# Summing and turning the modulation vectors of a diffusion transformer: one transposing reduction and one 0/1 matmul in place of eight TensorE instructions

## Chip, cores, metric

The kernel runs on 1 core of one Trainium2 chip. The metric is device time in microseconds (us): the median of several executions. Beside them stands one profiled execution, from which all rows below come.

## What is computed

Two layers of a transformer for a diffusion generator, on 256 latent and 256 context tokens of 1024 features. Each layer has a first FFN, a mixer (two kinds of attention and a linear recurrence) and a second FFN; each of these shifts, scales and gates its input with modulation vectors. The part that matters here:

```python
m_lat = (jax.nn.silu(c) @ ada_w[l] + ada_b[l]).reshape(b, N_MOD, d_model)
m_ctx = (jax.nn.silu(c_ctx) @ ada_w[l] + ada_b[l]).reshape(N_MOD, d_model)
...
h = ffn_step(h, ml, ffn1_w13[l], ffn1_w2[l], norm_g[l, 0], 0)
```

N_MOD is 9, d_model 1024. So for each layer and each of nine indices m there is a product of two vectors (c and c_ctx) with a 1024 x 1024 block of `ada_w`, with a bias added.

## The kernel before

Features lie on the 128 partitions, tokens along the free dimension, 512 at a time (256 context, 256 latent). Every large fp32 product is made of three fp32r matmuls: ScalarE copies a weight tile into a high half (`split`, line 353), VectorE subtracts to get the low half (line 354), and `mm3` (lines 360 to 362) adds high x high, low x high and high x low. Names tell the place: `f_0a8L` is the low half of the first-product weights of FFN 0 (the first of the layer), first of the two gate halves, feature group 8; `f_0pa` and `f_0pb` are the accumulators of the two gate halves; `f_0w_4L` is a low half of the second product's weights (`project_back`), `f_0w0y` its accumulator, `f_0gH`/`f_0gL` the halves of its input. `f_2...` is the same for the second FFN.

Two of the first layer's vectors (m = 0 and 1) are made on TensorE at the start (`ada_start`). The other 16, (0, 2) to (0, 8) and (1, 0) to (1, 8), are made on VectorE beside the FFNs (`ada_mod`): four 1 MB loads of `ada_w` on the SP queue (tile `araw`, three buffers), and for each 128 rows of the block and each of the two vectors one multiply-add over 128 x 1024 elements (lines 225 and 227) into `aacc`, one buffer. `ada_mod` is a generator; the FFN takes one step of it after each feature group. At the end of each vector:

- four matmuls with a column of ones in a 128 x 32 block (`left1`) sum the accumulator over the partitions (line 233), each writing 32 of the 128 partitions of `asum`;
- `to_mods` copies that to SBUF on ScalarE (line 180), turns it in four 128 x 128 transposes on TensorE (line 183, `ada_..t`), and two VectorE adds with the bias write 128 x 8 each into `mods` (line 188).

Then `gain` or a multiplication by 0.5 follows. A scheduler puts the instructions into the engines' queues; each engine works its queue in order. The order around the change is thus the scheduler's, from the order in the code, its priorities and its own estimates of durations.

`rsqrt` (line 251) makes the small reciprocal roots of the norms, in a tile `r` of three buffers. `shape_constants` builds the table of constants, which is loaded at the start on the SP queue, the first 128 columns by themselves.

Of the kernel before, what the change touches and what calls it, by code (L numbers as in the profile page):

```python
# [10 lines left out]
F32 = mybir.dt.float32  # L11
F32R = mybir.dt.float32r
AF = mybir.ActivationFunctionType
ALU = mybir.AluOpType
AX = mybir.AxisListType
# [11 lines left out]
EPS = 1e-6  # L27
GRID_W = 64
THETA = 10000.0
C_IDENT, C_COS, C_SIN, C_LDA, C_LGQ = 0, 128, 384, 640, 768  # L30
C_ALL = 864
HALVES = ((0, 0, 256), (1, 256, 512))
FSPLIT = (0, 12, 22)
TAGS = {'e': 5, 'p': 5, 'v': 4, 'Q': 5, 'K': 4, 'o': 8, 'T': 6}
# [2 lines left out]
def shape_constants():  # L37

    out = np.zeros((128, C_ALL), np.float32)
    out[:, C_IDENT:C_IDENT + 128] = np.eye(128, dtype=np.float32)  # L40
    half = HD // 4
    inv = (np.float32(THETA) ** (-np.arange(half, dtype=np.float32) / np.float32(half))).astype(np.float32)
    t = np.arange(SEQ)
    pos = np.stack([t // GRID_W, t % GRID_W]).astype(np.float32)
    for p in range(128):
        axis, i = (p // 32) % 2, p % 16
        ang = (pos[axis] * inv[i]).astype(np.float32)
        out[p, C_COS:C_COS + SEQ] = np.cos(ang)
        out[p, C_SIN:C_SIN + SEQ] = np.sin(ang) * (-1.0 if p % 32 < 16 else 1.0)
    for h in range(4):  # L50
        out[:, C_LDA + 32 * h + h] = 1.0
    for i in range(3):
        out[:64, C_LGQ + 32 * i + 2 * i] = 1.0
        out[64:, C_LGQ + 32 * i + 2 * i + 1] = 1.0
    return out


@with_exitstack
def hybrid_kernel(ctx: ExitStack, tc, x, c, ctx_tok, c_ctx, ada_w, ada_b, norm_g, ffn1_w13, ffn1_w2,
# [3 lines left out]
    V, S, G, PE = nc.vector, nc.scalar, nc.gpsimd, nc.tensor  # L63
# [7 lines left out]
    sml = ctx.enter_context(tc.tile_pool(name="sml", bufs=4))  # L71
# [10 lines left out]
    def tabled(out_, in_, func, **kw):  # L82
        which = {AF.Tanh: AF.Exp}.get(func, func)
        if which != table["set"]:
            table.update(set=which, before=table["last"])
        i = S.activation(out_, in_, func, **kw)  # L86
        if table["before"] is not None:
            tc.add_manual_dep(i.ins, table["before"].name,
                              mybir.DependencyInfo(mybir.DependencyClass.NoSync, mybir.DependencyReason.DATA),
                              reason="table set")  # L90
        table["last"] = i.ins

    def t512(name="t"):
        return tmp.tile([128, 512], F32, tag="t", name=name)

    def ps(name="ps", tag="ms"):
        return pss.tile([128, 512], F32, tag=tag, name=name)
# [5 lines left out]
    start = ctx.enter_context(ExitStack())  # L103
# [7 lines left out]

    cs = cp.tile([128, C_ALL], F32, name="cs")
    nc.sync.dma_start(out=cs[:, 0:128], in_=consts[:, 0:128])
# [7 lines left out]
    bT = cp.tile([128, L, 72], F32, name="bT")  # L121
# [41 lines left out]
    mods = [cp.tile([128, 72, 2], F32, name=f"mods{l}") for l in range(L)]  # L163
    gs = [cp.tile([128, 3, KD, 2], F32, name=f"gs{l}") for l in range(L)]

    def gain(l, i, k0, k1):

        n0 = col["ng"] + (3 * l + i) * KD
        V.scalar_tensor_tensor(
            gs[l][:, i, k0:k1], mods[l][:, 8 * (3 * i + 1) + k0:8 * (3 * i + 1) + k1, :], 1.0,  # L170
            vT[:, n0 + k0:n0 + k1].rearrange("p (k o) -> p k o", o=1).to_broadcast([128, k1 - k0, 2]),
            op0=ALU.add, op1=ALU.mult)

    def to_mods(l, acc, m0, mstep, c0, off, what, more=None):


        nb = len(off)
        rows_ = 128
        sb = t512(f"{what}s")
        S.activation(sb[0:rows_, :], acc[0:rows_, :], AF.Copy)  # L180
        tp = ps(f"{what}t", "tp")
        for t in range(4):
            PE.transpose(tp[:, 128 * t:128 * t + rows_], sb[0:rows_, 128 * t:128 * t + 128], ident[0:rows_, 0:rows_])
        tv = tp.rearrange("p (t r) -> p t r", t=4)
        for b in range(nb):
            q = 8 * m0 + mstep * b + c0
            st_ = off[b][1] - off[b][0]
            V.tensor_tensor(
                out=mods[l][:, q:q + 4, :], in0=tv[:, :, off[b][0]:off[b][1] + 1:st_],
                in1=bT[:, l, q:q + 4].rearrange("p (t o) -> p t o", o=1).to_broadcast([128, 4, 2]), op=ALU.add)  # L190
            if more is not None:
                V.tensor_tensor(out=mods[l][:, q:q + 4, :], in0=mods[l][:, q:q + 4, :],
                                in1=tv[:, :, off[b][0] + more:off[b][1] + more + 1:st_], op=ALU.add)

    def ada_start(pool, part, acc):

# [13 lines left out]
    def ada_started(acc, part):  # L210
        to_mods(0, acc, 0, 8, 4 * part, ((0, 1), (32, 33)), f"ada_s{part}", 64)
        gain(0, 0, 4 * part, 4 * part + 4)

    def ada_mod(pool, l, m):


        acc = pool.tile([128, 2, 1024], F32, tag="aacc", name=f"aacc{l}_{m}", bufs=1)
        for n in range(4):
            w = pool.tile([128, 2, 1024], F32, tag="araw", name=f"araw{l}_{m}_{n}")
            nc.sync.dma_start(out=w, in_=ada_w[l, 256 * n:256 * n + 256, 1024 * m:1024 * m + 1024].rearrange("(n p) c -> p n c", p=128))  # L220
            for i in range(2):
                k = 2 * n + i
                for v in range(2):
                    if k == 0:
                        V.tensor_scalar(acc[:, v], w[:, i], cpad[:, k, v:v + 1], None, op0=ALU.mult)
                    else:
                        V.scalar_tensor_tensor(acc[:, v], w[:, i], cpad[:, k, v:v + 1], acc[:, v], op0=ALU.mult, op1=ALU.add)  # L227
            yield
        sm = ps(f"asum{l}_{m}")
        for v in range(2):  # L230
            for b in range(2):
                j = 2 * b + v
                PE.matmul(sm[32 * j:32 * j + 32, :], left1, acc[:, v, 512 * b:512 * b + 512], start=True, stop=True)
        to_mods(l, sm, m, 4, 0, ((0, 32), (64, 96)), f"ada{l}_{m}")
        if m % 3 == 1:
            gain(l, m // 3, 0, KD)
        elif m != 5 and m % 3 == 2:
            V.tensor_scalar(mods[l][:, 8 * m:8 * m + 8, :], mods[l][:, 8 * m:8 * m + 8, :], 0.5, None, op0=ALU.mult)
# [3 lines left out]
    left1 = cs[:, C_LDA:C_LDA + 32]  # L242
# [5 lines left out]

    def rsqrt(st, scale, a, b, name):
        sl = slice(a // 4, b // 4)  # L250
        r = sml.tile([128, 128], F32, tag="r", name=name, bufs=3)
        tabled(r[sl], st[sl, 0:128], AF.Sqrt, bias=eps_t[sl], scale=scale)
        V.reciprocal(r[sl], r[sl])
        return r
# [13 lines left out]
    class Stat:  # L268
# [31 lines left out]
        def rstd(self, a, b):  # L300
            if self.c0:
                r = self.scales(a, b)
                bc = ps(f"bc{self.name}_{a}")
                for n in range((b - a) // 128):
                    PE.matmul(bc[:, a + 128 * n:a + 128 * n + 128], r[:, n:n + 1].to_broadcast([128, 128]), ident,
                              start=True, stop=True)
                return bc
            st = ps(f"st{self.name}_{a}", "tp")
            parts = [self.sum, self.sq[6], self.sq[7]]
            for n, sq in enumerate(parts):  # L310
                stat_mm(st, left1, sq, a, b, n == 0, n == 2)
            r = rsqrt(st, 1.0 / D, a, b, f"r{self.name}_{a}")
            return spread(ps(f"bc{self.name}_{a}"), r, 0, 1, a, b, a, b)
# [108 lines left out]
    def ffn(l, i, w13, w2, c0, nstat, adas=(), begin=None):  # L422
        nm = f"f{l}_{i}"
        with tc.tile_pool(name=f"gp{nm}", bufs=1) as gp, tc.tile_pool(name=f"ap{nm}", bufs=3) as ap:
            opening = begin is not None
            def run_adas():
                if opening:
                    small_params()
                for l_, m in adas:
                    yield from ada_mod(ap, l_, m)  # L430
# [71 lines left out]
    def mixer(l, c0, nstat):  # L502
        W = w_in[l]
        nm = f"m{l}"
        with tc.tile_pool(name=f"mp{l}", bufs=1) as mp, tc.tile_pool(name=f"mt{l}", bufs=1) as mt:
# [262 lines left out]
            def subln(heads):  # L768
                st = ps(f"{nm}ost")
                for n, h in enumerate(heads):  # L770
                    sq = t512("sq")
                    S.activation(sq[:, c0:], om[h][:, c0:], AF.Square)
                    stat_mm(st, cs[:, C_LDA + 32 * n:C_LDA + 32 * n + 32], sq, c0, NT, n == 0, n == len(heads) - 1)
                ro = rsqrt(st, 1.0 / 128, c0, NT, f"{nm}ro")
                for n, h in enumerate(heads):
                    bc = spread(ps(f"{nm}obc{h}"), ro, n, 1, c0, NT, c0, NT)
                    V.scalar_tensor_tensor(om[h][:, c0:], om[h][:, c0:], gsub[:, l:l + 1], bc[:, c0:], op0=ALU.mult, op1=ALU.mult)
# [191 lines left out]
```

## Time and profile before

| | |
|---|---|
| median of 3 runs | 1788.25 us (1787.35 to 1788.76) |
| profiled execution | 1787.78 us, of which 1786.0 us are the span of the profile |
| TensorE matmul busy | 1753.0 us, 98% |
| TensorE weight loads busy | 1465.0 us, 82% |
| VectorE busy | 1129.4 us, 63% |
| ScalarE busy | 714.0 us, 40% |
| GpSimd busy | 77.7 us, 4% |
| moved by DMA | 249.33 MB, mean 140 GB/s |

The span is the part of an execution between the first and the last instruction of the profile. Matmuls are pipelined: a row's duration is longer than the distance to the next, so the distance between starts is what a matmul costs its queue. An fp32 matmul shows as two records, an fp32 transpose or an fp32r matmul as one.

### The profile page before, as it was taken

How to read it: one execution, taken by the hardware profiler on the slowest of the kernel's cores; microseconds unless marked ns; L12 is line 12 of the kernel's file. 1: busy time of each engine (PE TensorE's matmuls, PEld its weight loads, DVE VectorE, ACT ScalarE, POOL GpSimd, SP SyncE). 2: the span in 40 equal slices, each digit the busy share in tenths (PEclk: the TensorE clock that was granted, in tenths of full speed). 3: DMA queues.
4: the chain of work that ended last, by engine and by line, in shares of the span. 5: the costliest groups of instructions: out<-in, count | busy, mean ns of one | idle time of the engine just before them, and what ended most of it. 6: DMA issues, size and time to landing. Idle time of an engine off the chain costs nothing.

```text
span 1786.0 us, 23865 instructions
## 1 busy us (share of the span) xinstructions
PE 1753.0 (98%) x9773; PEld 1465.0 (82%) x9773; DVE 1129.4 (63%) x1663; ACT 714.0 (40%) x1131; POOL 77.7 (4%) x75
## 2 busy tenths in 40 slices
PE   6999999999999999999999999999999999999998
PEld 3788888889787788878888898878888987799998
DVE  5767977337668767789566455783333777865554
ACT  3422222324677643221223342222222477754444
POOL 0000000001100010000000100000000120010001
PEclk9999999999999999999999999999999999999999
DMA  9555763233212136557355324552223322145652
GB/s 342 195 171 174 245 212 118 83 107 100 72 47 72 48 113 218 188 190 255 120 170 177 101 95 141 177 177 95 95 83 105 100 97 71 49 142 178 201 164 97
DMA packets 192822, 249.33 MB, mean 140 GB/s; under 512 B 6722, under 2 KB 170952, under 8 KB 192712
## 3 DMA queue, kind: packets, MB, share of 16 engines
q1 hardware_dynamic: 192712, 247.80, 41.6%
q8 instruction: 77, 1.26, 0.3%
q14 instruction: 33, 0.27, 0.0%
HBM read 246.73 MB, written 1.05 MB: 139 GB/s over the span
## 4 chain that ended last, share of the span: by engine, by line
PE 94%; DVE 2%; ACT 2%; issue 1%; DMA 0%; POOL 0%; SPq 0%; ACTq 0%; POOLq 0%; DVEq 0%
PE f_0pa L360 5%; PE f_0pa L361 5%; PE f_0pb L360 5%; PE f_0pa L362 5%; PE f_0pb L361 4%; PE f_0pb L362 4%; PE f_2pa L360 4%; PE f_2pb L360 3%; PE f_2pa L361 3%; PE f_2pa L362 3%; PE f_2pb L361 3%; PE f_2pb L362 3%; PE f_0w0y L360 3%; PE f_0w0y L362 2%; PE f_0w0y L361 2%; PE f_0w1y L360 2%
## 5 line engine op out<-in xcount | busy, mean ns | idle before, releaser
L227 DVE SCALAR_TENSOR_TENSOR aacc<-araw,cpad,aacc 128x1024 f32<-128x1024 f32 x224 | 275.0, 1276 | 2.8 <-DMA araw<-in_ada_w_dram 2.8
L86 ACT ACTIVATE g<-f_0pa 128x512 f32<-128x512 f32 x44 | 26.3, 598 | 153.3 <-PE f_0pa L362 153.3
L284 POOL TENSOR_TENSOR sss<-sss,sqs 128x512 f32<-128x512 f32 (+1 forms) x20 | 27.1, 1353 | 1322.4 <-ACT sqs L282 1321.7
L488 DVE TENSOR_TENSOR g<-g,f_0pb 128x512 f32<-128x512 f32 x44 | 30.1, 685 | 82.8 <-PE f_0pb L362 72.2
L354 DVE TENSOR_TENSOR f_0w_0L<-f_0w,f_0w_0H 128x1024 fp32r<-128x1024 f32 (+1 forms) x32 | 34.7, 1088 | 55.4 <-ACT f_0w_0H L353 55.3
L353 ACT ACTIVATE f_0w_0H<-f_0w 128x1024 fp32r<-128x1024 f32 (+1 forms) x32 | 30.4, 951 | 88.6 <-PE f_0w0y L362 39.8
L86 ACT ACTIVATE g<-f_2pa 128x512 f32<-128x512 f32 (+1 forms) x44 | 21.6, 490 | 106.0 <-PE f_2pa L362 106.0
L354 DVE TENSOR_TENSOR f_2w_0L<-f_2w,f_2w_0H 128x1024 fp32r<-128x1024 f32 (+1 forms) x32 | 34.9, 1089 | 36.0 <-ACT f_2w_0H L353 35.9
L326 ACT ACTIVATE xH<-xn,mods 128x256 fp32r<-128x256 f32 x88 | 39.0, 499 | 43.0 <-DVE xn L325 42.8
L353 ACT ACTIVATE f_2w_0H<-f_2w 128x1024 fp32r<-128x1024 f32 (+1 forms) x32 | 30.4, 950 | 64.2 <-PE f_2w0y L362 30.6
L360 PE MATMUL f_0w0y<-f_0gH,f_0w_0H 128*128 128x512 f32 x128 | 50.6, 397 | 0.0
L361 PE MATMUL f_0w0y<-f_0gH,f_0w_0L 128*128 128x512 f32 x128 | 50.3, 393 | 0.0
L362 PE MATMUL f_0w0y<-f_0gL,f_0w_0H 128*128 128x512 f32 x128 | 50.0, 391 | 0.0
L681 DVE TENSOR_REDUCE sm<-s 128x1 f32<-128x512 f32 (+1 forms) x72 | 42.1, 590 | 6.3 <-PE s L676 5.9
L488 DVE TENSOR_TENSOR g<-g,f_2pb 128x512 f32<-128x512 f32 (+1 forms) x44 | 24.3, 552 | 34.1 <-PE f_2pb L362 29.0
L360 PE MATMUL f_2w0y<-f_2gH,f_2w_0H 128*128 128x512 f32 (+1 forms) x128 | 43.3, 338 | 0.0
L361 PE MATMUL f_2w0y<-f_2gH,f_2w_0L 128*128 128x512 f32 (+1 forms) x128 | 43.1, 336 | 0.0
L353 ACT ACTIVATE f_0w_4H<-f_0w 128x1024 fp32r<-128x1024 f32 x16 | 17.0, 1061 | 64.7 <-PE f_0w0y L362 27.6
L362 PE MATMUL f_2w0y<-f_2gL,f_2w_0H 128*128 128x512 f32 (+1 forms) x128 | 42.8, 335 | 0.0
L360 PE MATMUL f_0w1y<-f_0gH,f_0w_0H 128*128 128x512 f32 (+1 forms) x120 | 42.4, 354 | 0.0
L362 PE MATMUL f_0w1y<-f_0gL,f_0w_0H 128*128 128x512 f32 (+1 forms) x120 | 41.6, 347 | 0.0
L361 PE MATMUL f_0w1y<-f_0gH,f_0w_0L 128*128 128x512 f32 (+1 forms) x120 | 41.6, 347 | 0.0
(1416 smaller groups left out, 5865.9 us busy)
## 6 DMA issues: line engine op xcount, KB each, us to landing
araw<-in_ada_w_dram SPq DMA_DIRECT2D x64, 1024.0 KB
f_0a<-in_ffn_w_dram SPq DMA_DIRECT2D x22, 1024.0 KB
f_0b<-in_ffn_w_dram SPq DMA_DIRECT2D x22, 1024.0 KB
f_2a<-in_ffn_w_dram SPq DMA_DIRECT2D x22, 1024.0 KB
f_2b<-in_ffn_w_dram SPq DMA_DIRECT2D x22, 1024.0 KB
f_0w<-in_ffn_w_dram SPq DMA_DIRECT2D x16, 1024.0 KB
f_2w<-in_ffn_w_dram SPq DMA_DIRECT2D x16, 1024.0 KB
adas<-in_ada_w_dram SPq DMA_DIRECT2D x16, 512.0 KB
```

The lines of the kernel that those rows point to most:

```text
L86: i = S.activation(out_, in_, func, **kw)
L227: V.scalar_tensor_tensor(acc[:, v], w[:, i], cpad[:, k, v:v + 1], acc[:, v], op0=ALU.mult, op1=ALU.add)
L284: self.adder.tensor_tensor(out=self.sum[:, a:b], in0=self.sum[:, a:b], in1=sq[:, a:b], op=ALU.add)
L326: S.activation(xH[:, k, a:b], t[:, a:b], AF.Identity, bias=sh)
L353: S.activation(vH, src, AF.Copy)
L354: V.tensor_tensor(out=vL, in0=src, in1=f32(vH), op=ALU.subtract)
L360: PE.matmul(acc, aH, bH, start=first, stop=False)
L361: PE.matmul(acc, aL, bH, start=False, stop=False)
L362: PE.matmul(acc, aH, bL, start=False, stop=last)
L488: V.tensor_tensor(out=t_[:, c0:], in0=t_[:, c0:], in1=pb[:, c0:], op=ALU.mult)
L681: V.reduce_max(st_[:, 0:1], s[:, 0:nk], axis=AX.X, negate=True)
```

## The change

The four summing matmuls, the ScalarE copy and the four transposes go. In their place one VectorE instruction transposes each 32 x 32 block of the accumulator and sums it along its rows: of 2048 values on each partition remain 64 (`red`), for each group of 32 features the sum over the 32 partitions of a quadrant. One matmul with a 0/1 matrix (`C_S32`: 4 x 4 copies of the 32 x 32 unit matrix) adds the four quadrants and puts the result on all four, and four VectorE adds with the bias, one for each quadrant, write `mods`. The constants lose two unused columns of 32 and gain the 128 columns of the 0/1 matrix; `r` has two buffers. `to_mods` stays for the two vectors of the start, with its last argument now required.

```diff
-C_IDENT, C_COS, C_SIN, C_LDA, C_LGQ = 0, 128, 384, 640, 768
-C_ALL = 864
+C_IDENT, C_COS, C_SIN, C_LDA, C_LGQ, C_S32 = 0, 128, 384, 640, 704, 800
+C_ALL = 928
...
+    out[:, C_S32:C_S32 + 128] = np.tile(np.eye(32, dtype=np.float32), (4, 4))
...
-        sm = ps(f"asum{l}_{m}")
-        for v in range(2):
-            for b in range(2):
-                j = 2 * b + v
-                PE.matmul(sm[32 * j:32 * j + 32, :], left1, acc[:, v, 512 * b:512 * b + 512], start=True, stop=True)
-        to_mods(l, sm, m, 4, 0, ((0, 32), (64, 96)), f"ada{l}_{m}")
+        red = sml.tile([128, 64], F32, tag="red", name=f"red{l}_{m}", bufs=1)
+        V.tensor_reduce(red, acc.rearrange("p v (b j) -> p (v b) j", j=32), axis=AX.X, op=ALU.add, apply_transpose=True)
+        sm = ps(f"asum{l}_{m}")
+        PE.matmul(sm[:, 0:64], cs[:, C_S32:C_S32 + 128], red, start=True, stop=True)
+        sv = sm[:, 0:64].rearrange("p (v k r) -> p k v r", v=2, r=4)
+        for r in range(4):
+            q = slice(32 * r, 32 * r + 32)
+            V.tensor_tensor(
+                out=mods[l][q, 8 * m:8 * m + 8, :], in0=sv[q, :, :, r],
+                in1=bT[q, l, 8 * m:8 * m + 8].rearrange("p (k o) -> p k o", o=1).to_broadcast([32, 8, 2]), op=ALU.add)
...
-        r = sml.tile([128, 128], F32, tag="r", name=name, bufs=3)
+        r = sml.tile([128, 128], F32, tag="r", name=name, bufs=2)
```

The change also moves instructions. On TensorE, in the second product of layer 0's first FFN, at the end of vector (0, 4), the queue before reads:

```order
L362 MATMUL f_0w0y_1_0_1330<-f_0gL_304,f_0w_8_0H 128x512
L233 MATMUL asum_4_1409<-aacc_4_1225,cs 32x512 x4
L360 MATMUL f_0w0y_0_0_1451<-f_0gH_303,f_0w_0_0H 128x512
L361 MATMUL f_0w0y_0_0_1451<-f_0gH_303,f_0w_0_0L 128x512
L362 MATMUL f_0w0y_0_0_1451<-f_0gL_304,f_0w_0_0H 128x512
L360 MATMUL f_0w0y_1_0_1452<-f_0gH_303,f_0w_0_0H 128x512
L183 MATMUL ada_4t<-cs,ada_4s 128x128 x4
L361 MATMUL f_0w0y_1_0_1452<-f_0gH_303,f_0w_0_0L 128x512
```

And now, in the changed program, whose lines are five further down there:

```order
L367 MATMUL f_0w0y_1_0_1318<-f_0gL_304,f_0w_8_0H 128x512
L233 MATMUL asum_4_1399<-red_4_1397,cs 128x64
L365 MATMUL f_0w0y_0_0_1433<-f_0gH_303,f_0w_0_0H 128x512
L366 MATMUL f_0w0y_0_0_1433<-f_0gH_303,f_0w_0_0L 128x512
L367 MATMUL f_0w0y_0_0_1433<-f_0gL_304,f_0w_0_0H 128x512
L365 MATMUL f_0w0y_1_0_1434<-f_0gH_303,f_0w_0_0H 128x512
L366 MATMUL f_0w0y_1_0_1434<-f_0gH_303,f_0w_0_0L 128x512
```

The one matmul stands where the four stood, and the transposes are gone; the same holds at the other vectors.

On VectorE, around the start of that second product (the lines of `f_0w_..L` are the splits, `g` and `f_0gL` close a feature group of the first product, `aacc` are the vectors' multiply-adds), the queue before reads:

```order
L354 TENSOR_TENSOR f_0w_0_0L<-f_0w_0_1301,f_0w_0_0H 128x1024
L488 TENSOR_TENSOR g<-g,f_0pb_1181 128x512
L225 TENSOR_SCALAR aacc_4_1225<-araw_4_0_1226,cpad 128x1024
L490 TENSOR_TENSOR f_0gL_304<-g,f_0gH_303 128x512
L188 TENSOR_TENSOR mods_115<-ada_3t,bT 128x8 x2
L227 SCALAR_TENSOR_TENSOR aacc_4_1225<-araw_4_0_1226,cpad,aacc_4_1225 128x1024 x2
L227 SCALAR_TENSOR_TENSOR aacc_4_1225<-araw_4_1_1295,cpad,aacc_4_1225 128x1024 x4
L227 SCALAR_TENSOR_TENSOR aacc_4_1225<-araw_4_2_1303,cpad,aacc_4_1225 128x1024 x2
L488 TENSOR_TENSOR g<-g,f_0pb_1265 128x512
L354 TENSOR_TENSOR f_0w_0_4L<-f_0w_0_1301,f_0w_0_4H 128x1024
L227 SCALAR_TENSOR_TENSOR aacc_4_1225<-araw_4_3_1319,cpad,aacc_4_1225 128x1024 x4
L354 TENSOR_TENSOR f_0w_8_0L<-f_0w_8_1317,f_0w_8_0H 128x1024
```

And now:

```order
L227 SCALAR_TENSOR_TENSOR aacc_4_1213<-araw_4_3_1307,cpad,aacc_4_1213 128x1024 x3
L359 TENSOR_TENSOR f_0w_0_0L<-f_0w_0_1289,f_0w_0_0H 128x1024
L493 TENSOR_TENSOR g<-g,f_0pb_1175 128x512
L237 TENSOR_TENSOR mods_115<-asum_3_1207,bT 32x16 x4
L359 TENSOR_TENSOR f_0w_0_4L<-f_0w_0_1289,f_0w_0_4H 128x1024
L495 TENSOR_TENSOR f_0gL_304<-g,f_0gH_303 128x512
L231 TENSOR_REDUCE red_4_1397<-aacc_4_1213 128x64
L225 TENSOR_SCALAR aacc_5_1406<-araw_5_0_1407,cpad 128x1024 x2
L227 SCALAR_TENSOR_TENSOR aacc_5_1406<-araw_5_0_1407,cpad,aacc_5_1406 128x1024
L359 TENSOR_TENSOR f_0w_8_0L<-f_0w_8_1305,f_0w_8_0H 128x1024
```

Vector (0, 4)'s multiply-adds are done before the product starts, and the next vector's begin there; both splits have fewer of them in front. (Of the first list, rows between the ones shown are left out.)

## Rows read from the trace of the kernel before

**Rows 1.** The page, its first lines: span and busy time of each engine.
```profile
span 1786.0 us, 23865 instructions
...
PE 1753.0 (98%) x9773; PEld 1465.0 (82%) x9773; DVE 1129.4 (63%) x1663; ACT 714.0 (40%) x1131; POOL 77.7 (4%) x75
```
**Rows 2.** The page, the chain that ended last, by engine.
```profile
PE 94%; DVE 2%; ACT 2%; issue 1%; DMA 0%; POOL 0%; SPq 0%; ACTq 0%; POOLq 0%; DVEq 0%
```
**Rows 3.** Windows: length, busy time per engine, clock, DMA share, GB/s.
```profile
60.00:345.00 285.00, 285.00 (x1282) 229.40 (x1281) 205.99 (x251) 83.40 (x106) 0.00 (x0) 1.00 0.51 171
690.00:960.00 270.00, 270.00 (x1217) 217.52 (x1216) 199.27 (x215) 72.37 (x90) 0.00 (x0) 1.00 0.56 189
1060.00:1215.00 155.00, 155.00 (x703) 124.35 (x702) 103.41 (x114) 41.75 (x52) 0.00 (x0) 1.00 0.48 159
sum 710.00, PE 710.00 PEld 571.26 DVE 508.67 ACT 197.51 POOL 0.00; mean PE 236.67 PEld 190.42 DVE 169.56 ACT 65.84 POOL 0.00
```
**Rows 4.** Tile asum, TensorE: count, ns min/median/max, first and last start.
```profile
L233 PE MATMUL asum<-aacc,cs x128: 592/605/617, 121.0 to 1201.5; 128*32 128x512 f32 x128
```
**Rows 5.** Timeline of TensorE, vector (0, 4): start us, us, instruction.
```profile
194.96 0.40 PE L362 MATMUL f_0w0y<-f_0gL,f_0w_0H 128*128 128x512 f32 x1
195.28 1.06 PE L233 MATMUL asum<-aacc,cs 128*32 128x512 f32 x8
...
196.62 0.39 PE L361 MATMUL f_0w0y<-f_0gH,f_0w_0L 128*128 128x512 f32 x1
196.85 0.39 PE L362 MATMUL f_0w0y<-f_0gL,f_0w_0H 128*128 128x512 f32 x1
197.09 0.39 PE L360 MATMUL f_0w0y<-f_0gH,f_0w_0H 128*128 128x512 f32 x1
197.32 0.60 PE L183 MATMUL ada_4t<-cs,ada_4s 128*128 128x128 f32 x4
...
197.99 0.39 PE L362 MATMUL f_0w0y<-f_0gL,f_0w_0H 128*128 128x512 f32 x1
```
**Rows 6.** Timeline, TensorE, mixer of layer 0: two fp32 matmuls among weight matmuls.
```profile
594.93 0.40 PE L361 MATMUL m0oy<-xH,m0o_0L 128*128 128x512 f32 x1
...
595.16 0.64 PE L758 MATMUL o<-m0pT,m0v 128*128 128x128 f32 x4
...
595.88 0.28 PE L675 MATMUL s<-m0K,m0Q 128*128 128x256 f32 x1
```
**Rows 7.** Timeline, TensorE: a lone fp32 transpose between two weight groups.
```profile
76.70 0.39 PE L362 MATMUL f_0pb<-xL,f_0b2H 128*128 128x512 f32 x1
77.02 0.27 PE L141 MATMUL vps<-cs,rows 58*128 58x58 f32 x1
...
77.55 0.40 PE L361 MATMUL f_0pa<-xH,f_0a3L 128*128 128x512 f32 x1
```
**Rows 8.** Tile mods, VectorE: count, ns min/median/max, first and last start.
```profile
L188 DVE TENSOR_TENSOR mods<-ada_4t,bT x4: 155/160/165, 197.9 to 929.0; 128x8 f32<-128x8 f32 x4
```
**Rows 9.** Groups by form, VectorE: count, busy us, mean ns, idle before.
```profile
L681 DVE TENSOR_REDUCE sm<-s 128x1 f32<-128x512 f32 x48 | 32.4, 679 | 1.5 <-PE s L676 1.1
L681 DVE TENSOR_REDUCE sm<-s 128x1 f32<-128x256 f32 x24 | 9.6, 411 | 4.8 <-PE s L676 4.8
L253 DVE RECIPROCAL rs<-rs 64x128 f32<-64x128 f32 x8 | 7.6, 948 | 10.9 <-ACT rs L86 10.8
L497 DVE STREAM_SHUFFLE sh<-m0qr 128x256 f32<-128x256 f32 x8 | 3.6, 444 | 0.0
```
**Rows 10.** Timeline: a split on VectorE and the first matmul that reads it.
```profile
131.49 1.22 DVE L354 TENSOR_TENSOR f_0b8L<-f_0b,f_0b8H 128x1024 fp32r<-128x1024 f32 x1
...
139.12 0.39 PE L361 MATMUL f_0pb<-xH,f_0b8L 128*128 128x512 f32 x1
```
**Rows 11.** The same for a split at the start of the second product.
```profile
182.63 1.21 DVE L354 TENSOR_TENSOR f_0w_4L<-f_0w,f_0w_4H 128x1024 fp32r<-128x1024 f32 x1
...
184.43 0.39 PE L361 MATMUL f_0w0y<-f_0gH,f_0w_4L 128*128 128x512 f32 x1
```

More of the change, by code (lines that the diff above doesn't have):

```diff
@@ L49, in shape_constants @@
         out[p, C_SIN:C_SIN + SEQ] = np.sin(ang) * (-1.0 if p % 32 < 16 else 1.0)
-    for h in range(4):
+    for h in range(2):
         out[:, C_LDA + 32 * h + h] = 1.0
@@ L172, in gain, with to_mods @@
             op0=ALU.add, op1=ALU.mult)
-    def to_mods(l, acc, m0, mstep, c0, off, what, more=None):
+    def to_mods(l, acc, m0, mstep, c0, off, what, more):
         nb = len(off)
@@ L190, in to_mods @@
                 in1=bT[:, l, q:q + 4].rearrange("p (t o) -> p t o", o=1).to_broadcast([128, 4, 2]), op=ALU.add)
-            if more is not None:
-                V.tensor_tensor(out=mods[l][:, q:q + 4, :], in0=mods[l][:, q:q + 4, :],
-                                in1=tv[:, :, off[b][0] + more:off[b][1] + more + 1:st_], op=ALU.add)
+            V.tensor_tensor(out=mods[l][:, q:q + 4, :], in0=mods[l][:, q:q + 4, :],
+                            in1=tv[:, :, off[b][0] + more:off[b][1] + more + 1:st_], op=ALU.add)
     def ada_start(pool, part, acc):
```

## Prediction

> **What bounds the kernel now.** I read the totals first, then the chain of waits, then the three stretches in which the changed code runs. TensorE is busy 98% of a span of 1786.0 us [rows 1], and 94% of the chain that ended last is TensorE's own work [rows 2]. [...] So here a microsecond off TensorE's queue is a microsecond off the run, and a microsecond more on VectorE is free as long as no weight split comes late.
>
> The edited code runs once for each of 16 modulation vectors (seven of layer 0, nine of layer 1): 128 asum matmul records, two for each fp32 matmul, make 64 matmuls, four per vector [rows 4]. Rows 5 show what one vector costs TensorE. An undisturbed step from one 128x512 matmul to the next is 0.23 us (196.62 to 196.85).
>
> **What is removed from TensorE.** From the last weight matmul before the four asum matmuls (194.96) to the second one after them (196.62) it is 1.66 us, where two steps would be 0.46: they cost 1.20 us. Around the four transposes it is 0.90 us (197.09 to 197.99), again in place of 0.46: 0.44 us [rows 5]. I take the same for all 16, since shapes and neighbours repeat: 16 x 1.64 = 26.2 us. All of it is on the path.
>
> **What is added on TensorE.** One fp32 matmul for each vector, full 128x128 weights, 64 columns, at the place where the four asum matmuls stood. No row has this shape. Two fp32 matmuls of 128 columns with the same size of weights take 0.95 us from the step before to the one after (594.93 to 595.88), so 0.49 for two, 0.25 for one [rows 6]; if only columns counted, half of that, 0.12. A lone fp32 transpose between two weight groups, on a 58-row slice, takes 0.85 (76.70 to 77.55) less 0.46, so 0.39 [rows 7]; it changes the shape of the weights, as the asum matmuls do, and the new matmul doesn't. I take 0.25, the row with the same weights, and keep 0.12 and 0.39 as ends: 16 x 0.25 = 4.0 us (1.9 to 6.2).
>
> **VectorE.** Two adds of 0.16 us [rows 8] become four on 32 partitions each, which I put at 0.16 too; and there is the reduction of 2048 elements per partition. TENSOR_REDUCE takes 0.411 us for 256 and 0.679 us for 512 elements, thus 1.05 ns per element and some 0.14 fixed [rows 9]; 2048 make 2.3 us. That bound has no transposition in it. The shuffle of 256 fp32 columns takes 0.444 us [rows 9], hardly more than the reduction of as many, so moving data inside a 32-partition block has no visible surcharge; the upper end goes by the slowest VectorE row per element, RECIPROCAL with 0.948 us for 128 [rows 9], which would make 15 us. I take 2.3, the same operation. At 2.3 us VectorE has 16 x (2.3 + 0.64 - 0.32) = 42 us more to do, in stretches where it idles 710 - 508.67 = 201 us [rows 3]. I cost it at nothing on the path. The cover is the lead of the weight splits: the low half of f_0b8 is ready at 132.71 (131.49 + 1.22) and first used at 139.12, a lead of 6.4 us [rows 10]. If the cover were gone, TensorE would wait for the split.
>
> [...]
>
> **What moves.** The next vector's first products had to wait for the asum matmuls, which read the accumulator; now they wait for the reduction on their own queue. So VectorE starts each vector about one 128-feature group earlier, and the order listing shows the pieces spread between the splits. The place that was tightest was the start of the second FFN product: split f_0w_4L stood behind ten products, ended at 183.84 (182.63 + 1.21) and was used at 184.43, a lead of 0.6 us [rows 11]. In the new order it stands directly behind the previous vector's adds. The SP queue follows: the 1 MB loads of the vectors are issued ahead of one or two FFN weight loads that used to precede them, and each waits for a buffer that VectorE frees. One such load is about 6 us at 171 GB/s [rows 3]; with DMA at half load I cost it at nothing, covered by the same leads. POOL's queue is unchanged. ScalarE loses 16 copies that nobody on the path waits for: nothing. The shared buffers of r go from three to two; the third-last r is long read when the next one is written: nothing. The constants grow by 64 columns, 32 KB, on the queue ahead of the first vector's weights: 0.2 us at that same rate, taken in full.
>
> **The sum.** 26.2 - 4.0 - 0.2 = 22.0 us saved. The profiled execution took 1787.78 us and would take 1765.8; against the median of 1788.25 us it is **1766.2 us**. With the ends of the new matmul the saving is 19.8 to 24.1 us: 1764.2 to 1768.5 us.
>
> **The rivals.**
> - *Late weights at a few places.* The longer VectorE work, or an FFN load behind a vector's load, makes TensorE wait where leads are short: three second products run beside vectors (two in the first layer, one in the second), and a lead of 0.6 us against 2.3 us loses 1.7 us. Once each is 5 us: 1771 us. For it speaks the 0.6 us lead; against it, the new order takes just that split out from behind the products.
> - *VectorE becomes the bound, slower than before.* One mechanism: the transposing reduction is so slow that the splits queued behind it come later than the 6.4 us lead. From 6.4 us on, each further microsecond costs 16 us, and the saving is gone from 6.4 + 22/16 = 7.8 us. At the upper end of 15 us TensorE waits 16 x 8.6 = 138 us: 1766 + 138 = 1904 us. Against it speak the reduction and the shuffle at about 1 ns per element.
> - *No change.* The saved time comes back as TensorE waiting for the reduction: its matmul stands at a fixed place, and a reduction that is 1.4 us late each time gives back the 22 us: 1788 us. Against it: in the order VectorE has the next split and products behind the reduction before the group's matmuls end. That the edit does something else than it says is ruled out by the same listing: one reduction and one 64-column matmul for each vector, no transposes.
>
> **How the numbers follow.** A measurement of this kernel can tell about 0.2%, 3.6 us, from no change. Forecast 0.82, late weights 0.11, VectorE as the bound 0.04, no change 0.03. The forecast alone gives 1764.2 to 1768.5; to hold the time 8 times in 10 with some room for the spread of the runs (1787.35 to 1788.76) and for the case of late weights, the range is 1763.5 to 1771.5 us. Faster by over 0.2%: 0.82 + 0.11 = 0.93; within: 0.03; slower: 0.04.
>
> **What would show it.** Right: the two steps over the new matmul take 0.58 to 0.85 us in place of 1.66, no transposes behind it, TensorE still without idle time in the three stretches, the reduction near 2.3 us, and VectorE some 42 us busier. Wrong in size: another price of the lone matmul. Wrong in kind: TensorE idle ahead of a matmul that reads a low half (the splits are late) or ahead of asum (the reduction is late), or a reduction beyond 6 us.

## The result and the profile after

The changed kernel takes 1766.72 us (median of 4 runs, 1765.43 to 1767.22) where the kernel before, measured beside it, takes 1788.43 us (1787.35 to 1788.76): a ratio of 0.9879, with an interval of 0.9861 to 0.9896. The forecast was 1766.2 us. The profiled execution took 1765.43 us.

The page's first lines, beside [rows 1], and the engines of its chain, beside [rows 2]:

```profile
span 1763.7 us, 23533 instructions
...
PE 1732.0 (98%) x9613; PEld 1463.0 (83%) x9613; DVE 1171.9 (66%) x1711; ACT 707.3 (40%) x1115; POOL 77.8 (4%) x75
...
PE 94%; DVE 2%; ACT 2%; issue 1%; DMA 0%; POOL 0%; SPq 0%; ACTq 0%; POOLq 0%; DVEq 0%
```

TensorE has 21.0 us less to do and is still the bound, with the same shares; VectorE has 1171.9 - 1129.4 = 42.5 us more. The same three stretches as in [rows 3], with the same columns:

```profile
60.00:345.00 285.00, 285.00 (x1258) 234.89 (x1257) 225.57 (x272) 82.93 (x102) 0.00 (x0) 1.00 0.51 173
690.00:960.00 270.00, 270.00 (x1194) 223.09 (x1194) 232.69 (x250) 73.85 (x89) 0.00 (x0) 1.00 0.61 208
1060.00:1215.00 155.00, 155.00 (x686) 127.87 (x685) 97.16 (x115) 38.05 (x45) 0.00 (x0) 1.00 0.40 130
sum 710.00, PE 710.00 PEld 585.85 DVE 555.43 ACT 194.83 POOL 0.00; mean PE 236.67 PEld 195.28 DVE 185.14 ACT 64.94 POOL 0.00
```

TensorE (the first busy time) has no idle time in any of them, at a granted clock of 1.00; VectorE (the third) still idles 710 - 555.43 = 155 us. The new instructions, by tile, beside [rows 4] and [rows 8]:

```profile
L233 PE MATMUL asum<-red,cs x32: 217/247/274, 119.8 to 1179.0; 128*128 128x64 f32 x32
...
L231 DVE TRANSPOSE_TENSOR_REDUCE red<-aacc x16: 2302/2307/2312, 99.0 to 1156.6; 128x64 f32<-128x2048 f32 x16
```
```profile
L237 DVE TENSOR_TENSOR mods<-asum,bT x64: 151/170/180, 121.4 to 1180.6; 32x16 f32<-32x16 f32 x64
```

The transposing reduction takes 2.307 us. And the end of vector (0, 4) in TensorE's timeline, beside [rows 5]:

```profile
190.98 0.40 PE L367 MATMUL f_0w0y<-f_0gL,f_0w_0H 128*128 128x512 f32 x1
191.21 0.33 PE L233 MATMUL asum<-red,cs 128*128 128x64 f32 x2
191.35 0.48 PE L365 MATMUL f_0w0y<-f_0gH,f_0w_0H 128*128 128x512 f32 x1
191.67 0.40 PE L366 MATMUL f_0w0y<-f_0gH,f_0w_0L 128*128 128x512 f32 x1
```

The two steps over the new matmul take 191.67 - 190.98 = 0.69 us in place of 1.66; at the 16 vectors they take 0.678 to 0.694 us, mostly 0.679. Less two steps of 0.23 that is 0.22 us for each. The transposes are gone without a gap in their place. So the account closes: in the trace of before the four matmuls cost 1.650 to 1.664 less 0.46, the transposes 0.898 to 0.911 (once 1.016) less 0.46 us, in all about 16 x 1.64 = 26.2 us; less 16 x 0.22 = 3.5 makes 22.7, and the span is 1786.0 - 1763.7 = 22.3 us shorter.

### The profile page after: what moved, and what is told of

Same layout as the page of the kernel before. It is cut to its first block, busy times and chain, and to the rows that moved or that the text cites. A ratio compares the mean times of both kernels' runs of the same rounds, so it can differ in the third digit from the quotient of the medians.

```text
span 1763.7 us, 23533 instructions
## 1 busy us (share of the span) xinstructions
PE 1732.0 (98%) x9613; PEld 1463.0 (83%) x9613; DVE 1171.9 (66%) x1711; ACT 707.3 (40%) x1115; POOL 77.8 (4%) x75
## 3 DMA queue, kind: packets, MB, share of 16 engines
HBM read 246.76 MB, written 1.05 MB: 141 GB/s over the span
## 4 chain that ended last, share of the span: by engine, by line
PE 94%; DVE 2%; ACT 2%; issue 1%; DMA 0%; POOL 0%; SPq 0%; ACTq 0%; POOLq 0%; DVEq 0%
PE f_0pa L365 5%; PE f_0pa L366 5%; PE f_0pa L367 5%; PE f_0pb L365 5%; PE f_0pb L366 5%; PE f_0pb L367 5%; PE f_2pa L365 4%; PE f_2pb L365 4%; PE f_2pa L366 3%; PE f_2pa L367 3%; PE f_2pb L366 3%; PE f_2pb L367 3%; PE f_0w0y L365 3%; PE f_0w0y L367 3%; PE f_0w0y L366 3%; PE f_0w1y L365 2%
## 5 line engine op out<-in xcount | busy, mean ns | idle before, releaser
L359 DVE TENSOR_TENSOR f_0w_4L<-f_0w,f_0w_4H 128x1024 fp32r<-128x1024 f32 x16 | 19.5, 1221 | 33.4 <-ACT f_0w_4H L358 33.4
```

The lines of the kernel that those rows point to most:

```text
L359: V.tensor_tensor(out=vL, in0=src, in1=f32(vH), op=ALU.subtract)
```

## The experiments

The question was not whether the time fell, but why: whether the gain is TensorE's queue alone, how it divides, and what covers the work on VectorE. Each run computes all that the kernel computes; what is added in it changes nothing in the output. "Against changed" is the difference of the medians to 1766.72 us. The kernel before, measured again beside each group of runs, came out at 1787.77 to 1788.71 us, so a difference of under 1 us says nothing.

| run | us | ratio to before, interval | against changed |
|---|---|---|---|
| old TensorE work added back | 1791.80 | 1.0018 (1.0008 to 1.0027) | +25.1 |
| the four matmuls alone added back | 1785.03 | 0.9977 (0.9967 to 0.9988) | +18.3 |
| new matmul twice | 1768.94 | 0.9894 (0.9879 to 0.9908) | +2.2 |
| before with two buffers of r | 1788.44 | 1.0000 (0.9990 to 1.0009) | (before) |
| reduction twice | 1766.64 | 0.9878 (0.9863 to 0.9892) | -0.1 |
| reduction four times | 1770.41 | 0.9900 (0.9883 to 0.9916) | +3.7 |
| reduction six times | 1811.77 | 1.0141 (1.0121 to 1.0162) | +45.1 |
| one long reduction, shared buffer | 1856.84 | 1.0382 (1.0366 to 1.0397) | +90.1 |
| plain reduction, shared buffer | 1765.85 | 0.9877 (0.9860 to 0.9893) | -0.9 |
| reciprocal of 928 behind the reduction | 1769.44 | 0.9897 (0.9883 to 0.9912) | +2.7 |
| reciprocal of 464 behind the reduction | 1765.64 | 0.9876 (0.9861 to 0.9891) | -1.1 |
| long piece ahead of the matmul | 1791.03 | 1.0014 (1.0004 to 1.0024) | +24.3 |

**Where the gain lies.** The old TensorE work was put back into the changed kernel, with VectorE's new work kept: four fp32 matmuls of 32 x 512 and four transposes per vector, into a tile that nobody reads.

```diff
         PE.matmul(sm[:, 0:64], cs[:, C_S32:C_S32 + 128], red, start=True, stop=True)
+        rb = red.rearrange("p (o c) -> p o c", o=1).to_broadcast([128, 8, 64])
+        dm = ps(f"dmm{l}_{m}", "tp")
+        for j in range(4):
+            PE.matmul(dm[32 * j:32 * j + 32, :], left1, rb, start=True, stop=True)
+        dt = ps(f"dtr{l}_{m}", "tp")
+        for t in range(4):
+            PE.transpose(dt[:, 128 * t:128 * t + 128], cs[:, 128:256], ident)
```

> The changed kernel with the removed TensorE work put back as work without use: behind the new matmul four 32x512 fp32 matmuls on the reduced tile and four 128x128 transposes of constants for each vector. The output does not use them; VectorE's order, loads and waits stay nearly as changed. Theory (the gain is TensorE's queue time and nothing else): 16 x (1.20 + 0.44) = 26.2 us more than the changed kernel, 1766.7 + 26.2 = 1793 us, which is the time before plus the 3.6 us of the new matmul. Rival (some of the gain comes from the smoother order on VectorE and SP): clearly below 1790 us.

Measured: 1791.80 us. The groups by form show the work to be the old one (592 to 617 ns and 0.60 us in [rows 4] and [rows 5]):

```profile
L237 PE MATMUL dmm<-red,cs 128*32 128x512 f32 x128 | 18.1, 605 | 0.0
L240 PE MATMUL dtr<-cs 128*128 128x128 f32 x64 | 9.6, 272 | 0.0
```

VectorE's work is that of the changed kernel (552 us in the stretches beside 555) and its order nearly so, and yet the whole gain is gone, with 3.3 us on top of the 1788.51 us of before beside it, for the new matmul, which is still there. So nothing but TensorE's queue time pays: the other things that the change moves are worth nothing that can be seen. TensorE had no idle time in the stretches before either [rows 3], so there was no wait there that a better order could have taken away.

**How it divides.** The same without the last three added lines:

> As the first, with the four matmuls alone. Theory: 16 x 1.20 = 19.2 us more than the changed kernel, 1786 us; the difference to the first run is the transposes, 7 us. Rival: less, since a matmul could slip into idle time.

Measured: 1785.03 us, 18.3 more than the changed kernel, where 16 x 1.20 = 19.2 were predicted for the four matmuls; the transposes make up the other 6.8 us, where 16 x 0.44 = 7.0 were predicted.

**The price of the new matmul.** A second one into the same tile, with the same operands:

```diff
         PE.matmul(sm[:, 0:64], cs[:, C_S32:C_S32 + 128], red, start=True, stop=True)
+        PE.matmul(sm[:, 0:64], cs[:, C_S32:C_S32 + 128], red, start=True, stop=True)
```

> The changed kernel with the new 64-column matmul done twice. By the changed kernel's profile (two steps over it take 0.68 us in place of 0.455, so 0.22 us each) 16 x 0.22 = 3.6 us more if its price is the same behind itself: 1770.3 us. If most of that price is the entry into fp32 work and out of it, the second is cheaper: 1768 us.

Measured: 1768.94 us. TensorE's timeline at vector (0, 4):

```profile
191.64 0.40 PE L368 MATMUL f_0w0y<-f_0gL,f_0w_0H 128*128 128x512 f32 x1
191.87 0.33 PE L233 MATMUL asum<-red,cs 128*128 128x64 f32 x2
192.04 0.39 PE L234 MATMUL asum<-red,cs 128*128 128x64 f32 x2
192.24 0.48 PE L366 MATMUL f_0w0y<-f_0gH,f_0w_0H 128*128 128x512 f32 x1
192.56 0.40 PE L367 MATMUL f_0w0y<-f_0gH,f_0w_0L 128*128 128x512 f32 x1
```

The two steps now take 0.92 us instead of 0.69: the second costs 0.23 us like the first, 3.6 us in all. The span grew by 3.0 us, the median by 2.2, which the spread of the runs (2.5 us) does not separate from 3.6.

**The smaller buffer of r.** The kernel before, with `bufs=2` for `r` as its only edit:

> The kernel before with only the number of buffers of r changed from three to two. Theory: no difference, 1787 to 1790 us. Rival: a norm waits for its buffer, 1 us or more each time.

Measured: 1788.44 us beside 1788.71; no difference.

**What covers VectorE: one piece repeated.** The prediction's step was the lead: a split is ready 6.4 us before its use, so a longer piece of VectorE work makes it late from there on, 16 times over. The reduction was repeated, two, four and six times, each writing the same result:

```diff
         V.tensor_reduce(red, acc.rearrange("p v (b j) -> p (v b) j", j=32), axis=AX.X, op=ALU.add, apply_transpose=True)
+        V.tensor_reduce(red, acc.rearrange("p v (b j) -> p (v b) j", j=32), axis=AX.X, op=ALU.add, apply_transpose=True)
...
```

> The changed kernel with the transposing reduction done twice into the same tile, 37 us more on VectorE. Theory (VectorE's added work is hidden by the lead of the splits): within 0.2% of the changed kernel, 1765 to 1769 us, TensorE without idle time in the three stretches. Rival (the change already lives on the edge of VectorE's cover): 10 us or more on top.

> The reduction done four times, 9.2 us for each vector and 111 us more in all, against some 155 us that VectorE idles in the three stretches. By the step of the prediction on the lead (6.4 us): TensorE waits 16 x (9.2 - 6.4) = 45 us, 1811 us. Rival (the scheduler spreads the four between the splits, so that only VectorE's total counts): 1766 to 1772 us.

> The reduction done six times: 5 x 36.9 = 184 us more on VectorE than in the changed kernel, against 155 us that it idles in the three stretches. If VectorE's total is what decides, it no longer fits: at least 30 us of waiting on TensorE, 1790 to 1810 us, VectorE busy without a break in the stretches. By the lead of 6.4 us: 1767 + 16 x (13.8 - 6.4) = 1885 us. If the vectors can be finished later beside other stages: 1770 to 1780 us.

Measured: 1766.64, 1770.41 and 1811.77 us. The first two stretches and the sum, with four:

```profile
60.00:345.00 285.00, 283.40 (x1250) 233.00 (x1249) 262.17 (x290) 83.20 (x102) 0.00 (x0) 1.00 0.50 172
690.00:960.00 270.00, 269.34 (x1190) 221.93 (x1189) 265.25 (x261) 73.62 (x88) 0.00 (x0) 1.00 0.55 190
...
sum 710.00, PE 707.74 PEld 582.84 DVE 642.49 ACT 195.67 POOL 0.00; mean PE 235.91 PEld 194.28 DVE 214.16 ACT 65.22 POOL 0.00
```

With six, and below it TensorE's longest waits (who waits, for whom: us, times, longest):

```profile
60.00:345.00 285.00, 269.33 (x1159) 219.43 (x1158) 279.69 (x288) 77.44 (x94) 0.00 (x0) 0.97 0.49 167
690.00:960.00 270.00, 256.29 (x1111) 209.22 (x1111) 265.88 (x251) 68.54 (x82) 0.00 (x0) 0.97 0.48 164
```
```profile
PE f_0w0y L371 <- DVE f_0w_0L L364: 8.1, 2, 5.0
PE f_2w0y L371 <- DVE f_2w_0L L364: 7.7, 2, 7.4
PE f_0pa L371 <- DVE f_0a17L L364: 5.7, 1, 5.7
```

Four reductions are 9.2 us per vector, 2.8 over the lead, and cost 3.7 us instead of 16 x 2.8 = 45. They do not test the lead for one long piece, though: the scheduler puts the four apart, with other VectorE work between them, so that never more than two stand back to back (4.7 us). TensorE idles 2.3 us in the stretches. With six, VectorE would have 555 + 16 x 11.5 = 739 us to do in stretches of 710. It is busy 98% of the first two, TensorE waits for splits, and the time jumps. In these runs, where the work comes in pieces, it is the sum against the idle time that decides, and it decides late: 2.3 us more per vector cost nothing, 6.9 us 3.7, 11.5 us 45.

**One piece that cannot be divided.** The same 9.2 us as one instruction of 8.7: the accumulator is read four times over, and the 256 results need a larger tile, for which the shared 512-column buffers of the FFN were taken. The first 64 results are used, the rest is not.

```diff
-        red = sml.tile([128, 64], F32, tag="red", name=f"red{l}_{m}", bufs=1)
-        V.tensor_reduce(red, acc.rearrange("p v (b j) -> p (v b) j", j=32), axis=AX.X, op=ALU.add, apply_transpose=True)
+        red = t512(f"red{l}_{m}")
+        V.tensor_reduce(red[:, 0:256].rearrange("p (o g) -> p o g", o=4),
+                        acc.rearrange("p v (o b j) -> p o (v b) j", o=1, j=32).to_broadcast([128, 4, 64, 32]),
+                        axis=AX.X, op=ALU.add, apply_transpose=True)
```

> One transposing reduction for each vector that reads the accumulator four times over (8192 elements per partition, 256 results, the first 64 used): the same VectorE time as four reductions, about 9 us, but in one piece that no split can pass. By the prediction's step on the lead (each microsecond above 6.4 us costs 16): 1767 + 16 x 2.8 = 1811 us. Theory after the four reductions (1770 us; what counts is whether VectorE's total fits, and a piece of 9 us is shorter than most leads): 1768 to 1776 us, with the waits at a few splits.

Measured: 1856.84 us; neither theory had it. The reduction, the first two stretches, and waits of TensorE:

```profile
L231 DVE TRANSPOSE_TENSOR_REDUCE red<-aacc x16: 8701/8705/8706, 113.7 to 1270.3; 128x256 f32<-128x8192 f32 x16
```
```profile
60.00:345.00 285.00, 260.37 (x1099) 210.79 (x1098) 241.31 (x253) 72.36 (x89) 0.00 (x0) 0.95 0.47 161
690.00:960.00 270.00, 247.21 (x1103) 204.14 (x1102) 233.61 (x226) 65.88 (x82) 0.00 (x0) 0.95 0.51 176
```
```profile
PE f_0w0y L368 <- DVE f_0w_0L L361: 20.0, 4, 8.0
PE f_2w0y L368 <- DVE f_2w_0L L361: 9.6, 3, 4.7
...
PE f_2pa L368 <- DVE f_2a7L L361: 4.5, 1, 4.5
```

VectorE is 85 to 87% busy, not full, and TensorE waits for splits all the same. The first reduction starts at 113.7 us where it started at 99.0: the order is another one. What made the longest wait, 8.0 us for a split that begins at 191.49, stands in the queues of ScalarE and VectorE:

```profile
182.93 1.06 ACT L360 ACTIVATE f_0w_0H<-f_0w 128x1024 fp32r<-128x1024 f32 x1 [3.95 <-issue]
```
```profile
185.51 6.06 DVE L227 SCALAR_TENSOR_TENSOR aacc<-araw,cpad,aacc 128x1024 f32<-128x1024 f32 x5
191.49 1.22 DVE L361 TENSOR_TENSOR f_0w_0L<-f_0w,f_0w_0H 128x1024 fp32r<-128x1024 f32 x1
```

The high half was ready at 182.93 + 1.06 = 183.99, but the split stands in VectorE's queue behind the current vector's multiply-adds; the reduction is not among what it waits behind. TensorE waits over 1 us for a low half 14 times in this run, 58 us together. At all 14 such multiply-adds stand between the ready high half and its split, at eight the end of a reduction too. Nine times VectorE itself idles, up to 2.6 us, at its adds until the new matmul has run. So the late splits are late by their place in the queue. Four more runs asked what of the edit brings this about.

The shared buffer without the length, that is the changed kernel's own reduction writing into `t512(...)[:, 0:64]`:

> The changed kernel, but the reduction (single, 2.3 us) writes its 64 results into one of the shared 512-column buffers (tag t), which the FFN's g uses too, as in the run with one long reduction. No work is added. In the VectorE queue the order listing shows the reduction of vector (0, 2) moved from in front of split f_0b6L to behind split f_0b7L, and the next vector's products behind it. If it was the place and the shared buffer that made the long reduction cost 90 us: the first splits after the reductions are late here too, TensorE waits for low halves in the three stretches, and the time is well above the changed kernel, 1785 us or more. If it was the length of the instruction: no TensorE waits of more than a few us and 1766 to 1770 us.

Measured: 1765.85 us, with TensorE busy 710.00 of 710 us in the stretches. The shared buffer and a later place of the reduction alone cost nothing. The order is still not that of the one long reduction: behind the first reduction, split f_0a8L follows directly here (117.4 us), and there only after the four adds and eight multiply-adds (136.8 us).

The length without the shared buffer, first behind the reduction, as a reciprocal in place of 928 elements of the accumulator, which are overwritten next, then with half as many:

```diff
         V.tensor_reduce(red, acc.rearrange("p v (b j) -> p (v b) j", j=32), axis=AX.X, op=ALU.add, apply_transpose=True)
+        V.reciprocal(acc[:, 0, 0:928], acc[:, 0, 0:928])
```

> The changed kernel with its own red buffer, and one unsplittable VectorE instruction more behind each reduction: a reciprocal of 928 of the accumulator's elements, in place, after which they are overwritten by the next vector, so the output stays as it is. By the row of RECIPROCAL before (0.948 us for 128 elements) an estimated 6.9 us; with the reduction a piece of 9.2 us in which no split can run, and 16 x 6.9 = 110 us more on VectorE, of 155 us idle: as much in all as the four reductions. Theory of the total: as the four reductions, 1766 to 1772 us. Theory of the lead (a piece longer than 6.4 us delays a split by the difference, 16 times): 16 x 2.8 = 45 us more, 1811 us. In between: the lead counts only at the vectors where the split behind the piece is due soonest.

> The same with 464 elements: an estimated 3.4 us, with the reduction a piece of 5.7 us, under the 6.4 us lead, and 55 us more on VectorE in all. Both the theory of the lead and that of the total: no TensorE waits to speak of, 1766 to 1768 us. More than 1775 would say that leads elsewhere are shorter than the one that the prediction read.

Measured: 1769.44 and 1765.64 us. The reciprocal by form, and the first two stretches with 928:

```profile
L231 DVE RECIPROCAL aacc<-aacc 128x928 f32<-128x928 f32 x16 | 95.1, 5947 | 0.2
```
```profile
60.00:345.00 285.00, 284.62 (x1254) 233.96 (x1253) 258.20 (x279) 83.65 (x103) 0.00 (x0) 1.00 0.50 172
690.00:960.00 270.00, 268.76 (x1187) 221.59 (x1187) 266.59 (x253) 72.94 (x88) 0.00 (x0) 1.00 0.58 198
```

It takes 5.95 us, less than the 6.9 estimated, and with the reduction 8.3 us per vector. The two are not one piece everywhere: at ten vectors the scheduler put a split between them, at six they stand back to back. For those six the lead theory would have 6 x 1.9 = 11 us; TensorE loses 1.6 us in the stretches.

Last, a long piece in the reduction's own buffer, one column wider, that the matmul has to wait for:

```diff
-        red = sml.tile([128, 64], F32, tag="red", name=f"red{l}_{m}", bufs=1)
-        V.tensor_reduce(red, acc.rearrange("p v (b j) -> p (v b) j", j=32), axis=AX.X, op=ALU.add, apply_transpose=True)
+        red = sml.tile([128, 65], F32, tag="red", name=f"red{l}_{m}", bufs=1)
+        V.tensor_reduce(red[:, 0:64], acc.rearrange("p v (b j) -> p (v b) j", j=32), axis=AX.X, op=ALU.add, apply_transpose=True)
+        V.tensor_reduce(red[:, 64:65], acc.rearrange("p v (o c) -> p o v c", o=1).to_broadcast([128, 3, 2, 1024]), axis=AX.XYZ, op=ALU.add)
...
-        PE.matmul(sm[:, 0:64], cs[:, C_S32:C_S32 + 128], red, start=True, stop=True)
+        PE.matmul(sm[:, 0:65], cs[:, C_S32:C_S32 + 128], red, start=True, stop=True)
```

> The changed kernel with its own red buffer, one column wider, and a second, plain reduction behind the first: the accumulator read three times over (6144 elements, at 1.05 ns an estimated 6.5 us) into that column, which the matmul reads with the other 64 and nothing uses. So as much VectorE time as in the one long reduction (8.7 us per vector, 102 us more in all) and, other than with the reciprocal, a long piece that the asum matmul waits for; the buffers are not shared. If the one long reduction cost 90 us because a long piece stands between the sum and its matmul, so that the matmul and the adds come later and the splits queued behind them are late: TensorE idle for tens of us in the stretches and 1800 us or more. If it took the shared buffer as well as the length: as with the reciprocal, some 2 us of idle time in the stretches and 1766 to 1772 us.

Measured: 1791.03 us, between the two. Its first two stretches and its two longest waits of TensorE in them:

```profile
60.00:345.00 285.00, 277.57 (x1205) 226.94 (x1205) 258.42 (x275) 80.33 (x98) 0.00 (x0) 0.98 0.49 168
690.00:960.00 270.00, 266.40 (x1164) 218.19 (x1163) 266.03 (x246) 70.17 (x84) 0.00 (x0) 0.99 0.57 196
```
```profile
PE f_0w0y L366 <- DVE f_0w_0L L359: 7.0, 2, 5.0
...
PE f_2w0y L366 <- DVE f_2w_0L L359: 2.9, 1, 2.9
```

VectorE is as busy as with the reciprocal (258 and 266 us), and yet TensorE idles 11.0 us in the stretches instead of 1.6. The longest pieces are alike too: 8.7 us where the two reductions stand back to back, at five vectors, and 6.5 us elsewhere. So neither the busy time nor the longest piece decides alone. At its three waits of over 1 us for a low half the high half had been ready for 5.7 to 9.9 us, and again multiply-adds stood in front of the split. That the matmul has to wait for the long piece is what the edit changes against the reciprocal; but the scheduler's order changes with it, and no run held the order fixed, so which of the two costs the time is not shown.

By TensorE's measured steps, waits and the slower steps after them (below) make 16.4 of the 26.0 us by which the span of this run is longer than the changed kernel's. Of the other 9.6, 7.6 are in the second products of the FFNs, whose matmuls follow each other a little more slowly outside those too (`f_0w0y`: 233.4 ns on average instead of 230.1, gaps left out); why is open. The one long reduction's 90 us are thus narrowed, not settled: neither the shared buffer with a short reduction nor a long piece behind the reduction brings them, a long piece ahead of the matmul brings a part, and in the traces the waits come from splits queued behind multiply-adds.

No further version was run for speed: what is left of the change on TensorE is the new matmul, 3.6 us in all.

## Why the prediction was right, and the step that was wrong

- **What is removed:** 16 x 1.64 = 26.2 us from two distances in one timeline. Right: the trace of before has the same distances at the other vectors, within 0.02 us but for one of 1.02, and adding the work back costs 25.1 us, 18.3 and 6.8 for its two parts.
- **The new matmul:** 0.25 us taken, 0.12 to 0.39 as ends; 0.22 measured. The row with the same size of weights was the right neighbour. Half of it, by columns alone, would have been wrong: 64 columns cost nearly as much as 128 (0.22 beside 0.25 us).
- **The reduction:** 2.3 us from plain reductions of 256 and 512 elements; 2.307 measured. Transposing on the way in costs nothing visible: from 2048 elements (2.307 us) to 8192 (8.705 us) each further one takes 1.04 ns, and in the plain reductions of [rows 9] 1.05 ns.
- **VectorE's extra work:** 42 us forecast, 42.5 measured, hidden. Right, and doubly so: even twice the reduction is hidden (1766.64 us beside 1766.72).
- **What moves:** no load and no split came late: TensorE is busy 710.00 of 710 us in the stretches. The constants' 32 KB, taken at 0.2 us, can't be seen: the first matmul of the first FFN starts at 28.8 us, before at 29.5. The r buffers cost nothing (1788.44 us beside 1788.71).
- **The rivals:** no late weights: TensorE has no gap in the stretches. No change: TensorE waits nowhere for the reduction.

**The wrong step** is the cover's size: "From 6.4 us on, each further microsecond costs 16 us, and the saving is gone from 6.4 + 22/16 = 7.8 us." It took one lead for the price at all 16 vectors. Where the reciprocal makes an unbroken piece of 8.3 us, at six vectors, this step gives 11 us, and TensorE lost 1.6. With one reduction of 8.7 us at all 16 it gives 16 x 2.3 = 37 us, and the run lost 90. So 6.4 us is not where a cost sets in, and 16 us per microsecond is not its size. The row read was also a short one: of 91 splits of the FFNs' first products in the stretches of the trace before, nine have a lead under 6.4 us, and the median is 12.4. The lead of [rows 10] belongs, besides, to the order of before. In the changed kernel the same split and its first use stand here, and below them those of [rows 11]:

```profile
122.19 1.23 DVE L359 TENSOR_TENSOR f_0b8L<-f_0b,f_0b8H 128x1024 fp32r<-128x1024 f32 x1
...
136.59 0.39 PE L366 MATMUL f_0pb<-xH,f_0b8L 128*128 128x512 f32 x1
```
```profile
165.11 1.23 DVE L359 TENSOR_TENSOR f_0w_4L<-f_0w,f_0w_4H 128x1024 fp32r<-128x1024 f32 x1
...
180.45 0.39 PE L366 MATMUL f_0w0y<-f_0gH,f_0w_4L 128*128 128x512 f32 x1
```

The first lead is now 136.59 - 123.42 = 13.2 us (6.4 before), the second 180.45 - 166.34 = 14.1 us (0.6 before), though VectorE does more. A lead is what the scheduler left over in one order, not a stock that the next order draws on. It was harmless here, since the reduction came out at 2.3 us. For the slow end (15 us) there is no run; the one of 8.7 us is already 68 us slower than the kernel before, so the rival's direction would probably stand, but not its sum.

## What to carry to other kernels

Where one engine was busy without a gap, as TensorE was here in 710 of 710 us, an edit was worth what it took off that engine's queue, and distances between neighbours in one timeline priced it to a few per cent (26.2 us, and 25.1 when the work was put back); a new shape was priced well by the row with the same weights (0.25 us, 0.22 measured), and not by its column count (0.12). Spare time on the other engine was to be counted over the stretch, as long as the added work came in pieces that the scheduler could set apart: with 155 us idle, 6.9 us more per vector cost 3.7 us in all. A single long piece whose result another engine waits for needs its own test: in the two runs that had one it cost 24.3 and 90.1 us. Leads read from the old order said little about the new one (6.4 us became 13.2, 0.6 became 14.1): look at what the new order puts in front of a split whose input is ready.

## What the runs showed of the hardware

In the run with the one long reduction a wait of TensorE cost more than its length. It waits 7.99 us for a split, and this follows (starts, durations):

```profile
192.76 0.80 PE L368 MATMUL f_0w0y<-f_0gH,f_0w_0L 128*128 128x512 f32 x1 [7.99 <-DVE f_0w_0L L361]
193.35 0.63 PE L369 MATMUL f_0w0y<-f_0gL,f_0w_0H 128*128 128x512 f32 x1
193.78 0.63 PE L368 MATMUL f_0w0y<-f_0gH,f_0w_0L 128*128 128x512 f32 x1
...
197.27 0.39 PE L368 MATMUL f_0w0y<-f_0gH,f_0w_0L 128*128 128x512 f32 x1
197.50 0.40 PE L369 MATMUL f_0w0y<-f_0gL,f_0w_0H 128*128 128x512 f32 x1
```

The windows around it, whose third number from the end is the granted clock:

```profile
184.00:193.00 9.00, 0.97 (x3) 0.53 (x4) 9.00 (x9) 0.51 (x1) 0.00 (x0) 0.64 0.45 158
193.00:197.00 4.00, 4.00 (x10) 3.16 (x11) 4.00 (x4) 0.00 (x0) 0.00 (x0) 0.52 0.98 365
197.00:201.00 4.00, 4.00 (x19) 3.25 (x18) 4.00 (x4) 0.95 (x1) 0.00 (x0) 1.00 0.34 101
```

After the wait the granted clock is 0.52 in the window, and the matmuls follow each other at 0.43 us instead of 0.23; from 197 us on it is 1.00, and the steps are 0.23 us again. The ten matmuls of that window thus lose about 2 us on top of the 8. Over the whole trace of that run, what distances of 0.6 us and more between starts have beyond an ordinary step of 0.23 us is 65.9 us more than in the changed kernel, and for those of 0.36 to 0.6 us, among them the steps of 0.43 us in the window at 0.52, it is another 23.9: together 89.8 of the 91.9 us by which its span is longer. With six reductions it is 32.7 and 10.4 of 45.0. With four, where no wait in the stretches is longer than 0.91 us, the steps of 0.36 to 0.6 us add nothing. The sum in the prediction for a lost cover, waits alone, would have been about a quarter too low even with the right waits.

The transposing reduction's rate also holds for a longer one: 8192 elements in 8.705 us beside 2048 in 2.307, 1.04 ns for each further element, as for the plain one of [rows 9].
